# Keeping a decoder's residual stream token-major: activations stationary in the projections that feed it

## The chip, the cores and the metric

The kernel runs on one core of one Trainium2 chip. The core has a matrix engine (TensorE, PE in the profile; its weight loads are listed apart as PEld), a vector engine (VectorE, DVE), an activation engine (ScalarE, ACT), GpSimd (POOL) and a sync engine (SyncE, SP) that here only issues transfers. They run side by side, each through its own queue in order, and wait for each other by semaphores. SBUF is the working memory with 128 partitions; TensorE writes its results to PSUM, eight banks of 128 partitions x 512 f32.

The metric is device time of one execution in microseconds. The profile comes from one execution of its own.

## What is computed

A two-layer decoder trunk on 256 tokens of width 2048, all f32. Cut to the structure:

```python
for i in range(2):
    h = rms_norm(x, attn_norm_w[i])
    if i == 0:
        x = x + mixer_a(h, a_w_qkv, a_w_o)              # stick-breaking attention, 16 heads of 128
    else:
        k, v = shared_kv_blocks(x, kv_norm_w, b_w_kv)   # rms_norm, one projection, rotary on K
        x = x + mixer_b(h, b_w_q, b_w_o, k, v)          # dilated windows, 3 groups of 4 heads
    x = x + conv_ffn(rms_norm(x, ffn_norm_w[i]), w_up, conv_w, conv_b, w_down)   # inner width 5632
    gate = sigmoid(rms_norm(x, ple_norm_w[i]) @ ple_w_gate[i])
    x = x + gate * (p[i] @ ple_w_proj[i])               # p: 256 features per token
return rms_norm(x, final_norm_w)

def rms_norm(x, w):
    return x * rsqrt(mean(x * x, axis=-1) + 1e-6) * w
```

The residual stream is `x`. Four kinds of projection end in it: the attention outputs (`a_w_o`, `b_w_o`), the feed-forward output (`w_down`) and the pair `ple_w_gate`, `ple_w_proj`.

## The kernel before

**Layout.** The stream is held transposed. `x[j]`, j = 0 to 15, is a tile of 128 features on the partitions x 256 tokens; the host hands `x` over transposed and turns the output back. Every activation is held in this form.

**Split operands.** Each f32 operand of a projection is split into a rounded part `hi` (type fp32r) and the rest `lo`. An activation tile `h` holds its hi in columns 0 to 255 and its lo in 256 to 511 (`split_x`, lines 130 to 140, which also multiplies the norm's gain in). A product is hi x hi + hi x lo + lo x hi.

**Weights.** `weights` (line 199) streams the matrix in strips of 512 output features: SP loads raw tiles of up to four blocks of 128 input features (1 MB, four buffers), then ScalarE writes `hi` (line 217) and VectorE `lo` (line 218), two blocks at a time, four buffers each. I call one block of 128 input features of one strip a k-step. `steps` (line 221) sets the order: two k-steps for each output in turn, with the last two k-steps of a strip sorted by output, so that outputs finish one after the other.

**Two forms of a projection.** `strip_t` (line 235) makes transposed results: the weights are stationary, the activations move. For each of four output blocks of 128 features it issues, for each k-step, one matmul with `hi` and 512 columns (line 244, activation hi and lo at once) and one with `lo` and 256 columns (line 247). The bank holds two halves that are added later. `strip_v` (line 265) makes token-major results: the activations are stationary, the weights move. For each of two tiles of 128 tokens it issues, for each k-step, three matmuls of 512 columns (lines 274 to 276) into one bank. Before the change only V used it. A third form, `strip_1` (line 250), is transposed with three matmuls of 256 columns and serves the small `wpp`.

**What follows a projection into the stream.** `add_blocks` (line 492) runs over four strips of `wo_a`, `wo_b` or one half of `wdn`: for each of the four blocks of a strip two VectorE adds into `x[j]` (lines 289 and 290), a square on ScalarE (line 165) added up on VectorE (line 169), and the split of the new block for the next projection. `ple` (line 561) does the gate: `strip_t` on `wpg`, `strip_1` on `wpp`, then `evac` (line 279: copy one half, add the other, multiply by rstd), sigmoid, product, add, square, split. The feed-forward runs in two halves: 6 pairs of up strips, four down strips over 24 k-steps, 5 pairs, four down strips over 20.

**Norm.** `Norm.add` sums squares per partition and token, `done` (line 172) sums over partitions by a matmul with ones (line 176), then Ln, Exp and one Newton step on 128 x 256 give `rstd` spread over all partitions; `column=True` turns it into one value per token on the partitions (line 192) for V. rstd is applied after the next projection.

**Start and end.** `load_x` (line 599) loads two blocks of the transposed stream for every two k-steps of the first strip. `late_loads` (line 114) issues constants on ACT's queue. At the end the last strip of the last gate is followed by the norm, then VectorE and GpSimd multiply eight tiles of 128 x 512 by rstd (line 634), and SP and ACT send them (line 635).

**Order.** The program is written out straight, and a scheduler places each engine's instructions by priority (the written order) and by when it expects their inputs, so that an instruction may go ahead of earlier ones on its engine. The weight splits have raised priority (`AHEAD`). Once placed, each engine's queue is fixed. PSUM: five banks for accumulators (`acc`), one for small products (`att`), a pair (`two`). Activations live in a ring of 42 tiles of 128 x 512.

Of the kernel before, what the change touches and what calls it, by code (L numbers as in the profile page):

```python
# [36 lines left out]
G_ATTN, G_FFN, G_PLE, G_KV, G_FIN = 0, 2 * KB, 4 * KB, 6 * KB, 7 * KB  # L37
V_CONV = 8 * KB
# [29 lines left out]
LAG = 2  # L68
# [5 lines left out]
def tile_trunk(ctx, tc, xT_d, pT_d, pos_d, vec_d, cst_d, csb_d, wqkv, wo_a, wkv, wq_b, wo_b, wup, wdn, wpg, wpp, out_d):  # L74
# [31 lines left out]
    x, x2 = [], []  # L106
    for j0 in range(0, KB, 2):
        t = cst.tile([P, 2, S], F32, name=f"x{j0}")
        x += [t[:, 0, :], t[:, 1, :]]
        x2.append(t)  # L110
# [34 lines left out]

    class Norm:

        def __init__(self):
            self.s = tt("ssum", bufs=2)  # L150
            self.n = 0
            self.rest = []
            self.table = None
# [6 lines left out]
        def add(self, src, apart=False):  # L160
            if self.n == 0:
                nc.scalar.activation(self.s, src, AF.Square)
            else:
                q = tt("sq", tag="t", bufs=6)
                nc.scalar.activation(q, src, AF.Square)
                if apart:
                    self.rest.append(q)
                else:
                    nc.vector.tensor_tensor(self.s, self.s, q, op=OP.add)
            self.n += 1  # L170

        def done(self, column=False):
            ps = bank("nrm")
            qs = [self.s] + self.rest
            for i, q in enumerate(qs):
                nc.tensor.matmul(ps[:, :S], ONE, q, start=i == 0, stop=i == len(qs) - 1)  # L176
            v = tt("nv", tag="t", bufs=6)
            nc.vector.tensor_scalar(v, ps[:, :S], 1.0 / D, EPS, op0=OP.mult, op1=OP.add)
            y = tt("ny", tag="t", bufs=6)
# [3 lines left out]
            t = tt("nt", tag="t", bufs=6)  # L183
# [3 lines left out]
            nc.vector.scalar_tensor_tensor(r, t, 1.5, y, op0=OP.add, op1=OP.mult)  # L187
            if not column:
                return r, None
            pc = bank("ncol")  # L190
            for t in range(2):
                nc.tensor.matmul(
                    pc[:, 2 * t : 2 * t + 1], r[0:1, t * P : (t + 1) * P], ONE[0:1, 0:1], start=True, stop=True
                )
            rc = tt("rcol", (P, 4), bufs=2)
            nc.vector.tensor_copy(rc[:, 0:4:2], pc[:, 0:4:2])
            return r, rc
# [52 lines left out]
    def strip_1(W, s, xs, two):  # L250

        n = len(xs)
        ps = [None] * 2
        a = dict(skip_group_check=True)
        for k, o, hi, lo in (g for group in steps(weights(W, s, n), n, 4) for g in group):
            if k == 0 and o % 2 == 0:
                ps[o // 2] = two[:, o // 2, :]
            c = slice(o * P, (o + 1) * P)
            d = ps[o // 2][:, (o % 2) * S : (o % 2 + 1) * S]
            nc.tensor.matmul(d, lo[:, c], xs[k][:, :S], start=k == 0 and o % 2 == 0, stop=False, **a)  # L260
            nc.tensor.matmul(d, hi[:, c], xs[k][:, S:], start=False, stop=False, **a)  # L261
            nc.tensor.matmul(d, hi[:, c], xs[k][:, :S], start=False, stop=k == n - 1, **a)  # L262
        return [ps[o // 2][:, (o % 2) * S : (o % 2 + 1) * S] for o in range(4)]

    def strip_v(W, s, xs):

        n = len(xs)
        ps = [None] * 2
        for k, t, hi, lo in (g for group in steps(weights(W, s, n), n, 2) for g in group):
# [18 lines left out]
    def add_to_x(j, ps):  # L288
        nc.vector.tensor_tensor(x[j], ps[:, :S], x[j], op=OP.add)  # L289
        nc.vector.tensor_tensor(x[j], ps[:, S:], x[j], op=OP.add)  # L290

    def v_tiles(ps, rc):
        out = []
        for t in range(2):
            v = rt("v")
            nc.scalar.activation(v, ps[t], AF.Copy, scale=rc[:, 2 * t : 2 * t + 1])
# [195 lines left out]
    def add_blocks(W, xs, bases, norm, base=0):  # L492
        out = [[] for _ in bases]
        for s in range(4):
            ps = strip_t(W, s, xs, base=base)
            if norm is None:
                for o in range(4):
                    add_to_x(4 * s + o, ps[o])
                continue
            if s == 3:  # L500
                norm.load_table()
            for o in range(4):
                j = 4 * s + o
                add_to_x(j, ps[o])
                norm.add(x[j])
                for lst, t in zip(out, split_x(x[j], j, bases)):
                    lst.append(t)
        return out

    def ffn(i, xs, rstd):  # L510
# [32 lines left out]
        add_blocks(wdn[i], gs, [], None)  # L543
# [4 lines left out]
        (h,) = add_blocks(wdn[i], gs, [G_PLE + i * KB], norm, base=4 * half)  # L548
# [12 lines left out]
    def ple(i, xs, ps_, rstd, norm, bases=None):  # L561
        out = []
        for s in range(4):
            end = bases is None and s == 3
            if end:
                pr = strip_1(wpp[i], s, ps_, two=two_banks())
            gp = strip_t(wpg[i], s, xs)
            if not end:
                pr = strip_1(wpp[i], s, ps_, two=two_banks())
# [6 lines left out]
            if s == 3 and not end:  # L576
                norm.load_table()
            for o, t in enumerate(ts):
                j = 4 * s + o
                nc.vector.tensor_tensor(t, pr[o], t, op=OP.mult)  # L580
                nc.vector.tensor_tensor(x[j], x[j], t, op=OP.add)
                norm.add(x[j], apart=end)
                if bases is None:
                    if not end:
                        nc.scalar.activation(x[j], x[j], AF.Copy, scale=gain(G_FIN, j))
                else:
                    out += split_x(x[j], j, bases)
        if bases is None:
            norm.load_table()
        return out  # L590
# [8 lines left out]
    def load_x(k0):  # L599
        nc.sync.dma_start(x2[k0 // 2], xT_d[:, k0 : k0 + 2, :])  # L600
# [116 lines left out]
```

## Time and profile before

| | us |
|---|---|
| median of 3 runs | 2391.64 (2391.57 to 2392.1) |
| profiled execution | 2391.75 |
| its span, first to last instruction | 2389.9 |
| mean granted TensorE clock | 0.997 |

Where the stages lie in the span, in us from its start, read from the timeline of PE:

| stage | from | to |
|---|---|---|
| first layer: mixer_a with its projections | 0 | 338 |
| wo_a | 338 | 411 |
| feed-forward | 411 | 1147 |
| ple | 1147 | 1254 |
| second layer: mixer_b with its projections | 1254 | 1462 |
| wo_b | 1462 | 1542 |
| feed-forward | 1542 | 2278 |
| ple | 2278 | 2371 |
| tail | 2371 | 2390 |

How to read the lines shown below: `L244 PE MATMUL acc<-h,whi 128*128 128x512` is line 244, an engine, an operation, the tile written and the tiles read (buffer numbers left out), the stationary operand's size and the moving one's. In the timeline the first column is the start in us, the second the time covered, and `x2` says that two like instructions in a row are merged. A matmul's recorded length goes beyond the start of the next one, so what a matmul costs PE is read from the distance between starts. In groups of instructions the part before the bar names the group and its count, then come busy time and mean ns of one, then the engine's idle time before them and what ended it. In the windows each engine has its busy us and, in brackets, its instructions, in the order PE, PEld, DVE, ACT, POOL; then come granted TensorE clock, DMA share and GB/s.

### The profile page before, as it was taken

To read this page: it belongs to the slowest core of one execution; us is meant where nothing else is said; L and a number is where in the kernel's file an instruction comes from. 1 tells how busy PE (TensorE), PEld (TensorE's weight loads), DVE (VectorE), ACT (ScalarE), POOL (GpSimd) and SP (SyncE) were. 2 spreads that over 40 slices of the span, in tenths; PEclk is the share of its full clock that TensorE was granted. 3 is DMA by queue.
4 is the path that set the end of the run, shared out by engine and by line. 5 is a ranking of instruction groups with operands and counts; after the bars stand their busy time and mean duration, and the time that the engine had idled before them with its cause. 6 is when DMAs were issued, how large, how long until landed. Compare 5 with 4: busy or idle time off the path is not lost.

```text
span 2389.9 us, 34074 instructions
## 1 busy us (share of the span) xinstructions
PE 2366.7 (99%) x13402; PEld 2049.5 (86%) x13402; DVE 1653.5 (69%) x2686; ACT 1283.9 (54%) x1877; POOL 3.6 (0%) x6
## 2 busy tenths in 40 slices
PE   8999999999999999999999999999999999999997
PEld 7888888888888888888888888888888888888886
DVE  8555557777765577766778876777776557776675
ACT  6555545655643455654665444565564345564564
POOL 0000000000000000000000000000000000000000
PEclk9999999999999999999999999999999999999998
DMA  7444455555555555555555444555555555555542
GB/s 279 163 170 167 170 176 188 187 194 188 184 193 193 181 190 193 187 186 191 178 194 191 171 151 164 190 194 188 185 192 193 182 189 194 187 185 192 185 169 105
DMA packets 64001, 439.86 MB, mean 184 GB/s; under 512 B 7232, under 2 KB 7392, under 8 KB 12128
## 3 DMA queue, kind: packets, MB, share of 16 engines
q1 hardware_dynamic: 62352, 435.19, 51.8%
q10 hardware_dynamic: 1488, 2.49, 0.3%
q8 instruction: 105, 1.72, 0.3%
q14 instruction: 56, 0.46, 0.1%
HBM read 435.55 MB, written 2.10 MB: 183 GB/s over the span
## 4 chain that ended last, share of the span: by engine, by line
PE 98%; DVE 1%; ACT 0%; DMA 0%; DVEq 0%; issue 0%; SPq 0%; ACTq 0%
PE acc L244 59%; PE acc L247 29%; PE accv L275 2%; PE accv L274 2%; PE accv L276 2%; PE po L304 1%; PE two L260 0%; PE two L261 0%; PE two L262 0%; PE two L362 0%; PE po L305 0%; PE nrm L176 0%; PE two L446 0%; PE two L376 0%; DMA x<-in_xT 0%; ACT whi L217 0%
## 5 line engine op out<-in xcount | busy, mean ns | idle before, releaser
L218 DVE TENSOR_TENSOR wlo<-raw,whi 128x1024 fp32r<-128x1024 f32 (+1 forms) x825 | 1007.0, 1222 | 650.0 <-ACT whi L217 644.4
L217 ACT ACTIVATE whi<-raw 128x1024 fp32r<-128x1024 f32 (+1 forms) x825 | 871.3, 1058 | 874.1 <-PE acc L244 734.3
L244 PE MATMUL acc<-h,whi 128*128 128x512 f32 x4224 | 1330.5, 396 | 8.1 <-DVE h L136 8.1
L247 PEld LDWEIGHTS acc<-h,wlo 128*128 128x128 f32 x4224 | 793.6, 188 | 186.0
L247 PE MATMUL acc<-h,wlo 128*128 128x256 f32 x4224 | 833.6, 279 | 0.0
L244 PEld LDWEIGHTS acc<-h,whi 128*128 128x128 f32 x4224 | 645.8, 189 | 9.2 <-DVE h L136 8.1
L244 PE MATMUL acc<-g,whi 128*128 128x512 f32 x1408 | 442.2, 396 | 0.0
L247 PEld LDWEIGHTS acc<-g,wlo 128*128 128x128 f32 x1408 | 264.2, 188 | 62.2
L247 PE MATMUL acc<-g,wlo 128*128 128x256 f32 x1408 | 276.4, 278 | 0.0
L244 PEld LDWEIGHTS acc<-g,whi 128*128 128x128 f32 x1408 | 214.7, 189 | 0.5 <-issue 0.4
L244 PE MATMUL acc<-o,whi 128*128 128x512 f32 x448 | 141.4, 397 | 0.0
L281 ACT ACTIVATE c<-acc 128x256 f32<-128x256 f32 x264 | 99.0, 375 | 48.5 <-PE acc L247 48.4
L282 DVE TENSOR_TENSOR c<-acc,c 128x256 f32<-128x256 f32 x264 | 105.1, 418 | 7.7 <-ACT c L281 7.7
L247 PEld LDWEIGHTS acc<-o,wlo 128*128 128x128 f32 x448 | 83.7, 188 | 19.1
L247 PE MATMUL acc<-o,wlo 128*128 128x256 f32 x448 | 88.9, 279 | 0.0
L274 PE MATMUL accv<-whi,h 128*128 128x512 f32 x224 | 88.5, 395 | 0.0
L275 PE MATMUL accv<-wlo,h 128*128 128x512 f32 x224 | 88.4, 394 | 0.0
L276 PE MATMUL accv<-whi,h 128*128 128x512 f32 x224 | 88.1, 393 | 0.0
L284 DVE TENSOR_TENSOR u<-c,rstd 128x256 f32<-128x256 f32 x176 | 71.9, 419 | 0.8
L143 ACT ACTIVATE g<-val 128x256 fp32r<-128x256 f32 x88 | 36.4, 414 | 66.0 <-DVE val L535 66.0
L244 PEld LDWEIGHTS acc<-o,whi 128*128 128x128 f32 x448 | 68.8, 189 | 0.5 <-issue 0.4
L289 DVE TENSOR_TENSOR x<-acc,x 128x256 f32<-128x256 f32 x96 | 38.1, 419 | 33.3 <-PE acc L247 33.3
(146 smaller groups left out, 1283.0 us busy)
## 6 DMA issues: line engine op xcount, KB each, us to landing
raw<-in_wup SPq DMA_DIRECT2D x176, 1024.0 KB, 4.8
raw<-in_wdn SPq DMA_DIRECT2D x88, 1024.0 KB, 4.8
raw<-in_wqkv SPq DMA_DIRECT2D x44, 1024.0 KB, 4.8
raw<-in_wpg SPq DMA_DIRECT2D x32, 1024.0 KB, 4.8
raw<-in_wkv SPq DMA_DIRECT2D x24, 1024.0 KB, 4.7
raw<-in_wo_a SPq DMA_DIRECT2D x16, 1024.0 KB, 4.8
raw<-in_wq_b SPq DMA_DIRECT2D x12, 1024.0 KB, 4.8
raw<-in_wo_b SPq DMA_DIRECT2D x12, 1024.0 KB, 4.8
```

The source lines that it names most:

```text
L143: nc.scalar.activation(h[:, :S], src, AF.Copy)
L217: nc.scalar.activation(hi[:, c], r, AF.Copy)
L218: nc.vector.tensor_tensor(lo[:, c], r, f32(hi[:, c]), op=OP.subtract)
L244: nc.tensor.matmul(ps[o], hi[:, c], xs[k], start=k == 0, stop=False)
L247: nc.tensor.matmul(ps[o][:, S:], lo[:, c], xs[k][:, :S], start=False, stop=k == n - 1)
L274: nc.tensor.matmul(ps[t], xl, hi, start=k == 0, stop=False)
L275: nc.tensor.matmul(ps[t], xh, lo, start=False, stop=False)
L276: nc.tensor.matmul(ps[t], xh, hi, start=False, stop=k == n - 1)
L281: nc.scalar.activation(c, ps[:, S:], AF.Copy)
L282: nc.vector.tensor_tensor(c, ps[:, :S], c, op=OP.add)
L284: nc.vector.tensor_tensor(out, c, rstd, op=OP.mult)
L289: nc.vector.tensor_tensor(x[j], ps[:, :S], x[j], op=OP.add)
```

## The change

The stream is kept as two tiles `x[t]` of 128 tokens on the partitions x 2048 features. The projections into it (`wo_a`, `wo_b`, `wdn`, `wpg`, `wpp`) use `strip_v`; `strip_1` is gone. After each strip of a projection that a norm follows, the new function `turn` transposes the strip on TensorE, eight 128 x 128 f32 transposes into the pair of banks `two`, and the split reads its blocks from there. The first half of `wdn` and the last `ple` have no `turn`.

A norm now sums along the free axis, by the accumulator of the square itself, and its small steps work on 128 x 2. Where the next projection is transposed, `done` spreads rstd by a diagonal matrix and a matmul with ones. The gate takes rstd as the scale of its sigmoid. The final gain, which lies along the free axis now, is loaded spread over the partitions. At the start the stream is loaded twice, transposed into ring tiles for the first projection and token-major into `x`; at the first `ple` copies of the transposed blocks are kept for the shared K/V. The output is token-major.

```diff
+        for t in range(2):
+            nc.scalar.dma_start(x[t], x_d[t])
+        nc.vector.tensor_copy(idf, IDB)
...
+    def strip_of(t, s):
+        return x[t][:, s * 512 : (s + 1) * 512]
...
+        def add(self, s, t):
+            q = tt("sq", (P, 768), tag="e", bufs=1)[:, :512]
+            nc.scalar.activation(q, strip_of(t, s), AF.Square, accum_out=self.s[:, t, s : s + 1])
+
+        def done(self, row=True):
+            small = lambda n: tt(n, (P, 2), bufs=2)
+            v = small("nv")
+            nc.vector.reduce_sum(v, self.s, axis=mybir.AxisListType.X)
+            nc.vector.tensor_scalar(v, v, 1.0 / D, EPS, op0=OP.mult, op1=OP.add)
...
+            rc = small("rcol")
+            nc.vector.scalar_tensor_tensor(rc, t, 1.5, y, op0=OP.add, op1=OP.mult)
+            if not row:
+                return None, rc
+            dg = tt("diag", tag="t", bufs=6)
+            for t in range(2):
+                nc.vector.tensor_scalar(dg[:, t * P : (t + 1) * P], idf, rc[:, t : t + 1], None, op0=OP.mult)
+            ps = bank("nrm")
+            nc.tensor.matmul(ps[:, :S], ONE, dg, start=True, stop=True)
             r = tt("rstd", bufs=2)
+            nc.scalar.activation(r, ps[:, :S], AF.Copy)
+            return r, rc
+
+    def turn(s):
+        two = two_banks()
+        out = []
+        for o in range(4):
+            d = two[:, o // 2, (o % 2) * S : (o % 2 + 1) * S]
             for t in range(2):
+                c = s * 512 + o * P
+                nc.tensor.transpose(d[:, t * P : (t + 1) * P], x[t][:, c : c + P], idf)
+            out.append(d)
+        return two, out
...
-    def add_blocks(W, xs, bases, norm, base=0):
-        out = [[] for _ in bases]
+    def add_strips(W, xs, gain_of, norm, base=0):
+        out = []
         for s in range(4):
-            ps = strip_t(W, s, xs, base=base)
-            if norm is None:
-                for o in range(4):
-                    add_to_x(4 * s + o, ps[o])
-                continue
-            if s == 3:
+            ps = strip_v(W, s, xs, base)
+            if norm is not None and s == 3:
                 norm.load_table()
-            for o in range(4):
-                j = 4 * s + o
-                add_to_x(j, ps[o])
-                norm.add(x[j])
-                for lst, t in zip(out, split_x(x[j], j, bases)):
-                    lst.append(t)
+            for t in range(2):
+                nc.vector.tensor_tensor(strip_of(t, s), ps[t], strip_of(t, s), op=OP.add)
+                if norm is not None:
+                    norm.add(s, t)
+            if norm is not None:
+                for o, b in enumerate(turn(s)[1]):
+                    out += split_x(b, 4 * s + o, [gain_of])
         return out
...
-    def ple(i, xs, ps_, rstd, norm, bases=None):
+    def ple(i, xs, ps_, rc, norm, gain_of=None):
...
-            gp = strip_t(wpg[i], s, xs)
+            gp = strip_v(wpg[i], s, xs)
             if not end:
-                pr = strip_1(wpp[i], s, ps_, two=two_banks())
+                pr = strip_v(wpp[i], s, ps_)
             ts = []
-            for o in range(4):
-                t = tt("pg", tag="t", bufs=6)
-                evac(gp[o], rstd, t)
-                nc.scalar.activation(t, t, AF.Sigmoid)
-                ts.append(t)
+            for t in range(2):
+                g = tt("pg", (P, 768), tag="w", bufs=2)[:, :512]
+                nc.scalar.activation(g, gp[t], AF.Sigmoid, scale=rc[:, t : t + 1])
+                ts.append(g)
...
+            for t, g in enumerate(ts):
+                nc.vector.tensor_tensor(g, pr[t], g, op=OP.mult)
+                nc.vector.tensor_tensor(strip_of(t, s), strip_of(t, s), g, op=OP.add)
+                norm.add(s, t)
+                if gain_of is None:
+                    nc.vector.tensor_tensor(strip_of(t, s), strip_of(t, s), gf[s], op=OP.mult)
+            if gain_of is not None:
+                two, bs = turn(s)
+                for o in range(0, 4, 2):
+                    r = rt("xT")
+                    nc.scalar.activation(r, two[:, o // 2], AF.Copy)
+                    raw += [r[:, :S], r[:, S:]]
+                    for q in range(2):
+                        out += split_x(bs[o + q], 4 * s + o + q, [gain_of])
...
     def load_x(k0):
-        nc.sync.dma_start(x2[k0 // 2], xT_d[:, k0 : k0 + 2, :])
-        for j in (k0, k0 + 1):
-            (h[j],) = split_x(x[j], j, [G_ATTN])
-        for j in range(k0 - LAG, k0 - LAG + 2):
-            if j >= 0:
-                norm.add(x[j])
+        t = rt("xT")
+        nc.sync.dma_start(t.rearrange("p (a b) -> p a b", a=2), xT_d[:, k0 : k0 + 2, :])
+        for q in range(2):
+            (h[k0 + q],) = split_x(t[:, q * S : (q + 1) * S], k0 + q, [G_ATTN])
...
-    r2 = rstd.unsqueeze(1).to_broadcast([P, 2, S])
-    for i, t in enumerate(x2):
-        eng = nc.gpsimd if i % 4 == 3 else nc.vector
-        eng.tensor_tensor(t, t, r2, op=OP.mult)
-        (nc.sync, nc.scalar)[i % 2].dma_start(out_d[:, 2 * i : 2 * i + 2, :], t)
+    for s in range(4):
+        for t in range(2):
+            c = strip_of(t, s)
+            if t == 0:
+                nc.vector.tensor_scalar(c, c, rc[:, t : t + 1], None, op0=OP.mult)
+            else:
+                nc.scalar.activation(c, c, AF.Copy, scale=rc[:, t : t + 1])
+            (nc.sync, nc.scalar)[t].dma_start(out_d[t][:, s * 512 : (s + 1) * 512], c)
```

More of the change, by code (lines that the diff above doesn't have):

```diff
@@ L73, in tile_trunk @@
 @with_exitstack
-def tile_trunk(ctx, tc, xT_d, pT_d, pos_d, vec_d, cst_d, csb_d, wqkv, wo_a, wkv, wq_b, wo_b, wup, wdn, wpg, wpp, out_d):
+def tile_trunk(ctx, tc, xT_d, x_d, pT_d, pos_d, vec_d, cst_d, csb_d, wqkv, wo_a, wkv, wq_b, wo_b, wup, wdn, wpg, wpp, gfin_d, out_d):
     nc = tc.nc
@@ L105, in tile_trunk @@
     vec = cst.tile([P, NVEC], F32, name="vec")
[L106 to L110, printed above, removed]
+    x = [cst.tile([P, D], F32, name=f"x{t}") for t in range(2)]
     c32 = cst.tile([P, NCST], F32, name="c32")
@@ L158, in load_table @@
             tc.keep_in_program_order(self.table)
[L160 to L179, printed above, removed]
+        def add(self, s, t):
[6 more added lines that the diff above has]
+            nc.vector.tensor_scalar(v, v, 1.0 / D, EPS, op0=OP.mult, op1=OP.add)
+            y = small("ny")
             with tc.issue_after(self.table.ins):
@@ L182, in done @@
                 nc.scalar.activation(y, y, AF.Exp, scale=-0.5)
-            t = tt("nt", tag="t", bufs=6)
+            t = small("nt")
             nc.vector.tensor_tensor(t, y, y, op=OP.mult)
             nc.vector.scalar_tensor_tensor(t, t, -0.5, v, op0=OP.mult, op1=OP.mult)
-            r = tt("rstd", bufs=2)
[L187 to L190, printed above, removed]
-            for t in range(2):
[L192 to L197, printed above, removed]
+            rc = small("rcol")
[7 more added lines that the diff above has]
+            nc.tensor.matmul(ps[:, :S], ONE, dg, start=True, stop=True)
+            r = tt("rstd", bufs=2)
+            nc.scalar.activation(r, ps[:, :S], AF.Copy)
[5 more added lines that the diff above has]
+            d = two[:, o // 2, (o % 2) * S : (o % 2 + 1) * S]
+            for t in range(2):
+                c = s * 512 + o * P
+                nc.tensor.transpose(d[:, t * P : (t + 1) * P], x[t][:, c : c + P], idf)
+            out.append(d)
+        return two, out
     def weights(W, s, n, fine=False, before=lambda k0: None, base=0):
@@ L248, in strip_t, with strip_v @@
         return ps
-    def strip_1(W, s, xs, two):
+    def strip_v(W, s, xs, base=0):
         n = len(xs)
         ps = [None] * 2
[L254 to L269, printed above, removed]
+        for k, t, hi, lo in (g for group in steps(weights(W, s, n, base=base), n, 2) for g in group):
             if k == 0:
@@ L547, in ffn @@
         norm = Norm()
-        (h,) = add_blocks(wdn[i], gs, [G_PLE + i * KB], norm, base=4 * half)
+        h = add_strips(wdn[i], gs, G_PLE + i * KB, norm, base=4 * half)
         return h, norm
@@ L576, in ple @@
-            if s == 3 and not end:
-                norm.load_table()
[L578 to L587, printed above, removed]
@@ L593, in tile_trunk @@
+            if gain_of is not None:
[6 more added lines that the diff above has]
+                        out += split_x(bs[o + q], 4 * s + o + q, [gain_of])
+        return out, raw
     idf = cst.tile([P, P], F32, name="idf")
@@ L599, in load_x @@
     def load_x(k0):
-        nc.sync.dma_start(x2[k0 // 2], xT_d[:, k0 : k0 + 2, :])
-        for j in (k0, k0 + 1):
-            (h[j],) = split_x(x[j], j, [G_ATTN])
-        for j in range(k0 - LAG, k0 - LAG + 2):
-            if j >= 0:
-                norm.add(x[j])
+        t = rt("xT")
+        nc.sync.dma_start(t.rearrange("p (a b) -> p a b", a=2), xT_d[:, k0 : k0 + 2, :])
+        for q in range(2):
+            (h[k0 + q],) = split_x(t[:, q * S : (q + 1) * S], k0 + q, [G_ATTN])
     first = strip_t(wqkv, 0, h, True, load_x)
     late_loads()
-    for j in range(KB - LAG, KB):
-        norm.add(x[j])
-    rstd, rc = norm.done(column=True)
+    for t in range(2):
+        for s in range(4):
+            norm.add(s, t)
+    rstd, rc = norm.done()
     o = mixer_a(h, rstd, rc, first)
-    nc.vector.tensor_copy(idf, IDB)
     for i in range(2):
         norm = Norm()
-        (h,) = add_blocks(wo_a if i == 0 else wo_b, o, [G_FFN + i * KB], norm)
+        h = add_strips(wo_a if i == 0 else wo_b, o, G_FFN + i * KB, norm)
         rstd, _ = norm.done()
@@ L703 @@
         "wpp": np.stack([_strips(w) for w in a["ple_w_proj"]]),
+        "gfin": np.ascontiguousarray(a["final_norm_w"]),
     }
@@ L714 @@
     o = r.results[0]["out_0"]
-    return np.ascontiguousarray(o.transpose(2, 1, 0).reshape(1, S, D))
+    return np.ascontiguousarray(o.reshape(1, S, D))
```

53 lines of the change are left out of this document (26 added, 27 removed).

## The prediction

> **What bounds the kernel now.** First the busy shares and the chain of work that ended last, then the waits of PE.
>
> ```profile
> PE 2366.7 (99%) x13402; PEld 2049.5 (86%) x13402; DVE 1653.5 (69%) x2686; ACT 1283.9 (54%) x1877; POOL 3.6 (0%) x6
> PE 98%; DVE 1%; ACT 0%; DMA 0%; DVEq 0%; issue 0%; SPq 0%; ACTq 0%
> ```
>
> ```profile
> PE acc L244 <- DVE h L136: 8.1, 1, 8.1
> PE nrm L176 <- ACT sq L165: 2.5, 2, 1.8
> ```
>
> PE carries the chain and waits for others 10.6 us in all, at the start and at the end. Neither a lighter VectorE nor a lighter ScalarE pays in between: only the number of PE instructions times their spacing counts, plus start and tail. Since recorded matmul durations overlap, I use spacings, the difference of start times in the timeline. First a stretch of L244/L247 pairs (transposed projection; columns: start, us, engine, line), then one of L274 to L276 (activations stationary, already used for V), then the first matmuls after an interruption.
>
> ```profile
> 1000.09 0.63 PE L244 MATMUL acc<-h,whi 128*128 128x512 f32 x2
> ...
> 1009.15 0.62 PE L244 MATMUL acc<-h,whi 128*128 128x512 f32 x2
> ```
>
> ```profile
> 153.29 0.39 PE L276 MATMUL accv<-whi,h 128*128 128x512 f32 x1
> ...
> 158.73 0.39 PE L276 MATMUL accv<-whi,h 128*128 128x512 f32 x1
> ...
> 1408.41 0.39 PE L276 MATMUL accv<-whi,h 128*128 128x512 f32 x1
> ...
> 1410.25 0.39 PE L275 MATMUL accv<-wlo,h 128*128 128x512 f32 x1
> ```
>
> Between the first two rows lie 13 groups of two 512-column and two 256-column matmuls: 9.06/13 = 0.697 us a group. A k-step (one block of 128 input features for four output blocks) is two groups, 1.394 us. Between the next two lie 24 matmuls: 5.44/24 = 0.2267 us each; a k-step of the other form is six, 1.360 us. Both stream 3,072 columns; the first needs eight instructions, the second six. The last pair, eight matmuls in 1.84 us, shows 0.230 us for the first ten or so after an interruption.
>
> **The change part by part.**
>
> *Projections.* The converted strips are those of wdn, wpg, wo_a and wo_b. Each of these transfers brings four k-steps:
>
> ```profile
> raw<-in_wdn SPq DMA_DIRECT2D x88, 1024.0 KB, 4.8
> raw<-in_wpg SPq DMA_DIRECT2D x32, 1024.0 KB, 4.8
> raw<-in_wo_a SPq DMA_DIRECT2D x16, 1024.0 KB, 4.8
> raw<-in_wo_b SPq DMA_DIRECT2D x12, 1024.0 KB, 4.8
> ```
>
> 148 transfers are 592 k-steps. 592 x (1.394 - 1.360) = 592 x 0.0338 (unrounded) = **-20.0 us**. At 0.230 throughout, a k-step would be 1.380 and the gain 8.2 us; I take the settled figure, since these strips are 72 to 144 matmuls with one group of transposes among them, and the row of 24 stands inside an unbroken run of 35.
>
> 0.697 against three times 0.2267 is 17 ns for one instruction fewer on the same 1,536 columns. The Trainium skill (TensorE: Matmul & The Clock Gate, Part 1) puts the fixed cost of a warm matmul at about 2.5 ns; by that, two instructions fewer save 5 ns a k-step, 3 us in all, and the sum below would be +11 instead of -6. The trace disagrees with its 17 ns; the rule is weighed among the rivals.
>
> wpp goes from 24 matmuls of 256 columns a strip to 12 of 512, in 8 strips:
>
> ```profile
> 1162.75 0.28 PE L262 MATMUL two<-p,whi 128*128 128x256 f32 x1
> ...
> 1163.83 0.28 PE L262 MATMUL two<-p,whi 128*128 128x256 f32 x1
> ```
>
> Nine in 1.08 us are 0.120 each: 8 x (24 x 0.120 - 12 x 0.2267) = **-1.3**.
>
> *Transposes.* `turn` runs for four strips of wo_a, wo_b, the second half of wdn in both layers, and the first ple: 20 times eight. The mixer's own f32 transposes show the price, in the midst of L274 to L276:
>
> ```profile
> 1421.14 0.39 PE L275 MATMUL accv<-wlo,h 128*128 128x512 f32 x1
> 1421.38 0.27 PE L482 MATMUL pt<-idf,e 128*128 128x128 f32 x1
> ...
> 1421.59 0.27 PE L484 MATMUL pt<-idf,e 128*128 128x128 f32 x1
> 1421.62 0.48 PE L276 MATMUL accv<-whi,h 128*128 128x512 f32 x1
> 1421.94 0.39 PE L274 MATMUL accv<-whi,h 128*128 128x512 f32 x1
> ```
>
> From L275 to L274 0.80 us pass where two spacings are 0.453: three transposes cost 0.347, with the return to the large matmuls in it; within the group they are 0.105 apart. Eight cost 0.347 + 5 x 0.105 = 0.87; times 20, **+17.4**. Afterwards nine matmuls at 0.230 instead of 0.2267: 0.03 x 20 = **+0.6**.
>
> A transpose waits for VectorE's add to the stream, and behind it on PE's queue stands the next strip, then everything. The order of issue is not the written one: L482 stands between L275 and L276 above, so the scheduler puts a transpose where it expects its input to be ready. How well, the first of the mixer's transposes shows:
>
> ```profile
> 1415.92 0.39 PE L276 MATMUL accv<-whi,h 128*128 128x512 f32 x1
> 1416.41 0.33 PE L482 MATMUL pt<-idf,e 128*128 128x128 f32 x1
> ```
>
> 0.49 instead of 0.227 is a stall of 0.26; the other group had none. So 0 to 0.26 a turn, 0 to 5.2 in all; I take 0.12: **+2.4**. The last turn of a stage is hidden: the next strip has 12 k-steps (16.7 us) before it needs the last four blocks, and add, transposes and split take about 3 to 5 us. Without that cover each of five ends would cost this much.
>
> *Norms.* Seven sums over partitions go; four diagonal products that spread rstd come (start, wo_a, wo_b, first ple).
>
> ```profile
> 32.73 0.39 PE L247 MATMUL acc<-h,wlo 128*128 128x256 f32 x2
> 32.97 0.59 PE L176 MATMUL nrm<-ssum,c 128*128 128x256 f32 x2
> ...
> 33.85 0.40 PE L247 MATMUL acc<-h,wlo 128*128 128x256 f32 x2
> ```
>
> 1.12 us where a group takes 0.70: 0.42 for one. Outside the tail six go and four come, and the two column turns (L192) go, whose price I set at about the same: (4 - 6 - 2) x 0.42 = **-1.7**; bounds -0.8 (L192 free) and -2.5. The vector work shrinks (two adds of 512 columns a strip for eight of 256, no rstd product at the gates) and is hidden by PE either way, as are the four loads of the final gain on ACT's queue, due only once the first strip of the last ple is added.
>
> *Start.* The stream now comes twice: transposed through the ring, and 2 x 1 MB in token rows, issued on ACT's queue behind L117.
>
> ```profile
> 10.00:15.00 5.00, 5.00 (x21) 4.40 (x20) 4.08 (x7) 4.19 (x8) 0.00 (x0) 1.00 1.04 405
> 25.00:30.00 5.00, 5.00 (x30) 4.34 (x30) 5.00 (x10) 3.54 (x9) 0.00 (x0) 1.00 1.03 423
> ```
>
> In these windows (last two columns: DMA share, GB/s) the DMA engines are full. The first strip eats 0.75 MB every 2.79 us, 269 GB/s. 2 MB more take 4.9 us at 410 GB/s; at half the rate each for 10 us the weights come 64 GB/s short, 2.4 us of PE. Bounds 0 (they land in prefetch slack) and 4.9 (all ahead of the weights): **+2.5**. That L169's 15 adds leave a VectorE that is busy 5.00 of 5 us here can only help.
>
> *Tail.* Now 18.6 us pass from the last projection's end to the end of the span, 2389.9:
>
> ```profile
> 2370.92 0.39 PE L247 MATMUL acc<-h,wlo 128*128 128x256 f32 x2
> ...
> 2380.59 5.84 DVE L634 TENSOR_TENSOR x<-x,rstd 128x512 f32<-128x512 f32 x6
> ```
>
> ```profile
> L296 ACT ACTIVATE v<-accv,rcol 128x512 f32<-128x512 f32 x14 | 9.6, 682 | 1.6 <-PE accv L276 1.6
> L157 ACT ACT_TABLE_LOAD x7 | 9.0, 1283 | 0.8 <-PEq L705 0.7
> L455 ACT ACTIVATION_READ_ACCUMULATOR e<-two,nmx 128x1 f32 x24 | 4.7, 195 | 0.0
> L218 DVE TENSOR_TENSOR wlo<-raw,whi 128x512 fp32r<-128x512 f32 x2 | 1.4, 692 | 5.5 <-ACT whi L217 5.5
> L454 DVE TENSOR_SCALAR nmx<-mx 128x1 f32<-128x1 f32 x24 | 3.6, 150 | 0.6
> L480 DVE TENSOR_SCALAR e<-e,co 128x256 f32<-128x256 f32 x12 | 4.2, 350 | 0.0
> ```
>
> After the last matmul come: sigmoid 0.68; table 1.28, beside product and add (2 x 0.69); two squares with their accumulator, 2 x 0.88, to about 3.7; the last gain product to 4.2; five small VectorE and two ScalarE steps, about 1.4, to 5.6; then four strips scaled and sent by each of two engines, VectorE 0.5 to 0.7 each, ScalarE 0.68 plus an issue of 0.3, to about 9.1; then what follows the last scaling now, 2389.9 - 2386.4 = 3.5: 12.6. **-6.0**; bounds -3 (every handover 0.2 us late) and -9 (squares beside the table load, scalings overlapped with issues).
>
> Sum: -20.0 - 1.3 + 17.4 + 0.6 + 2.4 - 1.7 + 2.5 - 6.0 = **-6.1**. The profiled execution took 2391.75 us with a span of 2389.9; less 6.1 it is 2385.65. The median of the runs, 2391.64, lies 0.11 below it: 2385.5, rounded **2385.6**.
>
> **The rivals.**
>
> *The transposes hold PE (slower).* If a turn's first transpose is issued right behind its strip, PE stands for the 0.69 us of the add, and for a weight split (1.22 us, VectorE's longest common operation) where that is ahead: 0.69 to 1.91 a turn, 13.8 to 38.2 in all in place of 2.4. With the middle, 26, the time is 2409. It decides against the change from (6.1 + 2.4)/20 = 0.43 us a turn. For it: PE takes its queue in order, and the add is one step off. Against it: the 0.00 and 0.26 us above. Chance 0.13.
>
> *The matmuls don't settle.* At 0.230 the gain of the projections shrinks from 20.0 to 8.2: 2397.4, just slower. For it: ten matmuls after each interruption are at that spacing. Against it: the long runs. If half of them settle, 2391.5. Chance 0.10, half of it slower.
>
> *The count of instructions saves nothing.* What costs 17 ns may be the change between 512 and 256 columns, or a weight load, and come back in these strips in another shape. At 0.697/3 = 0.2323 a matmul the projections gain 0: 2405.6, slower. Against it: the same weights, split and engine state already give 0.2267 at L274 to L276. Chance 0.02. By the page's 2.5 ns it would be 2402.6.
>
> *Small terms cancel.* Start +4.9, stalls 5.2, tail -3: +8.2 on the sum, 2393.8; with two of the three, about 2391. No difference. Nothing excludes it, as each end has a row behind it. Chance 0.25.
>
> *A transpose costs its record's length.* L484 is recorded at 0.27 us. If PE paid that for each, 160 x 0.27 = 43.2 in place of 17.4: 2411. Spacing 0.105 in the rows speaks against it, and this window of the transposes has granted clock 1.00 (the column after POOL):
>
> ```profile
> 1416.00:1462.00 46.00, 45.90 (x224) 37.14 (x223) 29.27 (x54) 18.94 (x26) 0.00 (x0) 1.00 0.46 159
> ```
>
> Chance 0.02. The Trainium skill (the same page, Part 4: PE-mode transpose) speaks for it: about 275 ns in one kernel's context, and a transpose doesn't count as activity for the clock. The trace agrees with the record's 0.27, not as a price in a row of transposes.
>
> **How the numbers follow.** The forecast as it stands, with its small terms near their values, has 0.48, from 2377 to 2390. By the bound of 0.2% (4.8 us, about what a measurement of this kernel tells from no change) faster is below 2386.9: two thirds or more of the forecast, and its luckier end (-16 with no stall, no start cost, tail -9: 2376), about 0.50 with what the other cases give. Slower is above 2396.4: 0.13 + 0.05 + 0.02 + 0.02, less what of the first lies below, 0.18. The rest, 0.32, is no difference. The range goes from the lucky end to just past the unsettled case, 2377 to 2399; beyond it stay some 0.05 below and 0.14 above.
>
> **What would show it.** In the changed profile: spacing of the strip matmuls in wdn 0.2267 (not 0.230); eight transposes in a group at 0.105 with no more than 0.3 us ahead of them; the first matmul still near 8.1 us and the first strip's end near 32; 12 to 13 us from the last matmul to the end; waits of PE for the stream's add near 2 us in total. It is wrong if PE's waits list the add with tens of us, if the transposes stand 0.2 us apart, or if the first strip ends 5 us late.

## The result, and the profile after

| | before | after |
|---|---|---|
| median, 7 runs each on one chip | 2391.59 (2391.18 to 2392.11) | 2399.31 (2397.34 to 2400.38) |
| profiled execution / its span | 2391.75 / 2389.9 | 2399.31 / 2397.5 |
| mean granted TensorE clock | 0.997 | 0.995 |

The changed kernel takes 1.0031 times as long (95% interval 1.0019 to 1.0042): 7.7 us slower, where 6 us faster was forecast. The busy shares and the chain of the changed kernel, and then its waits of PE (total us, times, longest):

```profile
PE 2363.2 (99%) x12260; PEld 2003.5 (84%) x12260; DVE 1561.1 (65%) x2364; ACT 1271.8 (53%) x1829; POOL 0.2 (0%) x4
PE 97%; ACT 1%; DMA 1%; DVE 1%; issue 0%; SPq 0%; ACTq 0%; DVEq 0%
```

```profile
PE acc L246 <- DVE h L134: 18.8, 5, 7.8
PE acc L249 <- DVE wlo L220: 0.7, 1, 0.7
...
PE two L197 <- DVE x L483: 0.2, 1, 0.2
```

PE is busy 3.5 us less and has 1,142 instructions fewer, as meant. The wait that the prediction feared most, L197's for the stream's add, is 0.2 us in the whole run. What grew is a wait of the first projection, for splits of the transposed stream: 8.1 us in one wait before, 18.8 in five now.

**Where the time went.** PE's timeline has two marks that both kernels share: the first attention scores (L362 before, L345 after) and the start of the last projection matmul.

```profile
57.15 0.59 PE L362 MATMUL two<-qk,qk 128*128 128x256 f32 x2
```

```profile
73.72 0.59 PE L345 MATMUL two<-qk,qk 128*128 128x256 f32 x2
...
2383.17 0.39 PE L263 MATMUL accv<-whi,h 128*128 128x512 f32 x1
```

Before, the second mark is the second of the two L247 that start at 2370.92, at 2371.04. So:

| part of the span | before | after | difference | forecast |
|---|---|---|---|---|
| start to first scores (head) | 57.15 | 73.72 | +16.6 | +2.1 |
| first scores to last projection matmul (middle) | 2313.9 | 2309.45 | -4.4 | -2.2 |
| from there to the end (tail) | 18.9 | 14.3 | -4.5 | -6.0 |

The forecast column is the prediction's own terms, put where they lie: its start term in the head, with -0.4 for the first norm, whose sum and column turn lie there (L176 at 32.97, L192 at 37.24); -20.0 - 1.3 + 17.4 + 0.6 + 2.4 - 1.3 in the middle. Middle and tail together gave 8.9 us, about what was forecast (8.2). The head alone turned the sign.

**What happened in the head.** From the transfers that SP issues in the first 40 us, before (L209 a weight, L600 two blocks of the stream):

```profile
...
1.65 0.42 SPq L600 DMA_DIRECT2D x<-in_xT  x1
2.12 0.43 SPq L209 DMA_DIRECT2D raw<-in_wqkv  x1
2.59 0.65 SPq L600 DMA_DIRECT2D x<-in_xT  x1
...
16.09 0.43 SPq L600 DMA_DIRECT2D x<-in_xT  x1
```

and after (L211 a weight, L591 the stream), with SP's largest wait in the first 60 us (total, times, longest):

```profile
...
1.64 0.42 SPq L591 DMA_DIRECT2D xT<-in_xT  x1
2.10 1.04 SPq L211 DMA_DIRECT2D raw<-in_wqkv  x2
5.12 0.33 SPq L591 DMA_DIRECT2D xT<-in_xT  x1
5.50 6.42 SPq L211 DMA_DIRECT2D raw<-in_wqkv  x4
14.09 0.33 SPq L591 DMA_DIRECT2D xT<-in_xT  x1
...
17.67 0.33 SPq L591 DMA_DIRECT2D xT<-in_xT  x1
...
27.59 0.42 SPq L591 DMA_DIRECT2D xT<-in_xT  x1
...
38.49 0.90 SPq L591 DMA_DIRECT2D xT<-in_xT  x2
```

```profile
SPq L211 <- DVE wlo L220: 34.7, 9, 9.1
```

Before, weight and stream loads alternate and the eighth stream load is out at 16.09. After, the scheduler put the second one behind two more weights, the third behind four, and so on. A weight load waits until VectorE's `wlo` frees a raw buffer; a stream load that needs no buffer stands behind it in SP's queue. The last leave at 38.49. PE then lacks activations while its weights lie ready:

```profile
17.55 1.22 PE L246 MATMUL acc<-h,whi 128*128 128x512 f32 x2 [4.93 <-DVE h L134]
...
21.56 0.80 PE L246 MATMUL acc<-h,whi 128*128 128x512 f32 x2
...
30.70 1.65 PE L246 MATMUL acc<-h,whi 128*128 128x512 f32 x3 [4.08 <-DVE h L134]
...
35.80 0.59 PE L184 MATMUL nrm<-diag,c 128*128 128x256 f32 x2
```

The brackets are idle time and what ended it. The idle time has a second price: after 4.93 us of it three groups take 4.01 us (17.55 to 21.56) in place of 3 x 0.697 = 2.09, after 4.08 us four take 5.10 (30.70 to 35.80) in place of 2.79. The windows show why (busy us of PE, PEld, DVE, ACT, POOL, then granted clock, DMA share, GB/s):

```profile
15.00:20.00 5.00, 2.45 (x7) 2.05 (x8) 2.02 (x3) 1.64 (x3) 0.00 (x0) 0.51 1.02 412
...
30.00:35.00 5.00, 4.30 (x13) 3.72 (x14) 2.73 (x11) 2.68 (x9) 0.00 (x0) 0.50 0.99 405
```

The granted clock is 0.51 and 0.50. The Trainium skill (TensorE: Matmul & The Clock Gate, Part 1) says that PE falls to half its clock after an idle window of about 3.4 us and regains it after as long a busy one; the trace agrees for idles of 4.93 and 4.08 us. Other runs give no length below which an idle is safe: in e8, below, one of 2.57 us was followed by half clock too, while in e3 the clock stayed at 1.00 after one of 2.80 us.

The head's account: waits 18.8 + 0.7 + 0.2 (one for `whi`) - 8.1 = 11.6 more; half clock 1.9 + 2.3 = 4.2. Against that, PE's first four groups, which start at half speed in both kernels (the first eight matmuls of 512 columns stand 0.45 us apart), took 4.8 us in place of 5.3, 0.5 less. So 1.3 of the 16.6 is not assigned.

### The profile page after: what moved, and what is told of

It reads as the page before. It is cut to its first block, busy times and chain, and to the rows that moved or that the text cites. A ratio compares the mean times of both kernels' runs of the same rounds, so it can differ in the third digit from the quotient of the medians.

```text
span 2397.5 us, 31193 instructions
## 1 busy us (share of the span) xinstructions
PE 2363.2 (99%) x12260; PEld 2003.5 (84%) x12260; DVE 1561.1 (65%) x2364; ACT 1271.8 (53%) x1829; POOL 0.2 (0%) x4
## 4 chain that ended last, share of the span: by engine, by line
PE 97%; ACT 1%; DMA 1%; DVE 1%; issue 0%; SPq 0%; ACTq 0%; DVEq 0%
PE acc L246 35%; PE acc L249 18%; PE accv L262 14%; PE accv L261 14%; PE accv L263 14%; PE two L197 1%; PE po L287 1%; DMA xT<-in_xT 1%; ACT whi L219 0%; DVE wlo L220 0%; DMA vec<-in_vec 0%; PE two L345 0%; PE po L288 0%; PE two L429 0%; PE two L359 0%
## 5 line engine op out<-in xcount | busy, mean ns | idle before, releaser
L246 PE MATMUL acc<-h,whi 128*128 128x512 f32 x3712 | 1174.8, 398 | 19.0 <-DVE h L134 18.8
L249 PEld LDWEIGHTS acc<-h,wlo 128*128 128x128 f32 x3712 | 698.8, 189 | 164.1 <-DVE wlo L220 1.1
L249 PE MATMUL acc<-h,wlo 128*128 128x256 f32 x3712 | 733.8, 279 | 0.7 <-DVE wlo L220 0.7
L262 PE MATMUL accv<-wlo,g 128*128 128x512 f32 x704 | 274.6, 390 | 0.0
L263 PE MATMUL accv<-whi,g 128*128 128x512 f32 x704 | 274.5, 390 | 0.0
L261 PE MATMUL accv<-whi,g 128*128 128x512 f32 x704 | 274.1, 389 | 0.0
L261 PE MATMUL accv<-whi,h 128*128 128x512 f32 x480 | 188.5, 393 | 0.0
L262 PE MATMUL accv<-wlo,h 128*128 128x512 f32 x480 | 188.5, 393 | 0.0
L263 PE MATMUL accv<-whi,h 128*128 128x512 f32 x480 | 188.1, 392 | 0.0
L263 PEld LDWEIGHTS accv<-whi,g 128*128 128x128 f32 x704 | 132.5, 188 | 26.9
L261 PEld LDWEIGHTS accv<-whi,g 128*128 128x128 f32 x704 | 132.2, 188 | 27.2
L262 PEld LDWEIGHTS accv<-wlo,g 128*128 128x128 f32 x704 | 132.2, 188 | 27.1
L263 PEld LDWEIGHTS accv<-whi,h 128*128 128x128 f32 x480 | 90.3, 188 | 17.8
L261 PEld LDWEIGHTS accv<-whi,h 128*128 128x128 f32 x480 | 90.2, 188 | 17.5
```

Source lines behind the costliest of these rows:

```text
L246: nc.tensor.matmul(ps[o], hi[:, c], xs[k], start=k == 0, stop=False)
L249: nc.tensor.matmul(ps[o][:, S:], lo[:, c], xs[k][:, :S], start=False, stop=k == n - 1)
L261: nc.tensor.matmul(ps[t], xl, hi, start=k == 0, stop=False)
L262: nc.tensor.matmul(ps[t], xh, lo, start=False, stop=False)
L263: nc.tensor.matmul(ps[t], xh, hi, start=False, stop=k == n - 1)
```

## The experiments

The theory: **SP's order** makes the head late. Its rival: the **second copy** of the stream, 2 MB of token rows, takes the DMA engines from the weights, as the prediction priced it. Beside them stood the question whether the **transposes** cost more than their spacing says. In all diffs "..." leaves something out; ratios are to the kernel before on the same chip.

### Order restored: e1_order

In the changed kernel each weight load of the first strip is issued behind the stream load that precedes it in the text. `issue_after` ties an instruction to another's place on the queue; the rest is unchanged.

```diff
-                nc.sync.dma_start(raw[...], W[...])
+                with tc.issue_after(xdma[0]) if fine and xdma[0] is not None else nullcontext():
+                    nc.sync.dma_start(raw[...], W[...])
...
-        nc.sync.dma_start(t.rearrange(...), xT_d[:, k0 : k0 + 2, :])
+        xdma[0] = nc.sync.dma_start(t.rearrange(...), xT_d[:, k0 : k0 + 2, :]).ins
```

> The changed kernel, with one thing undone: in the first strip each weight load on SP's queue is issued behind the transposed-stream load of the two blocks before it, so that weights and stream alternate as before the change; the 2 MB of token rows still load early on ACT's queue. Theory A (the order on SP's queue: stream loads stand behind weight loads that wait for a free buffer) expects the head, the time to the first attention scores, to fall from 73.7 us to 58 to 62 us and the whole from 2399.3 to 2384 to 2389. Theory B (the 2 MB fill the DMA engines) expects the head to stay above 68 us and the whole above 2393.

2387.04 us (2386.25 to 2389.26), ratio 0.9981 (0.9972 to 0.9990). First scores at 61.16, 12.6 earlier than in the changed kernel; the whole 12.3 faster. The waits of PE:

```profile
PE acc L249 <- DVE h L134: 10.1, 3, 7.9
PE nrm L184 <- DVE diag L182: 1.6, 2, 1.3
...
```

Behind the first groups the granted clock is 1.00 in every window of 4 us, from 12 to 40. So the order alone was worth some 12 of the 16.6 us, and the change with its start in order is faster than the kernel before.

### Rows late: e2_late_rows and e3_both

The token rows are loaded only behind the first strip's last split of the stream. e2 leaves SP's queue to the scheduler, e3 has the order of e1 as well.

```diff
-        for t in range(2):
-            nc.scalar.dma_start(x[t], x_d[t])
...
+            last[0] = nc.scalar.activation(h[:, :S], src, AF.Copy, scale=gain(b, j)).ins
...
+    with tc.issue_after(last[0]):
+        for t in range(2):
+            nc.scalar.dma_start(x[t], x_d[t])
```

> The changed kernel, but the 2 MB of token rows are issued only after the last split of the first strip's activations on ScalarE; the order on SP's queue is left to the scheduler, which still puts some weight loads ahead of stream loads (third stream load behind four weight loads in place of six). Theory B (contention with the 2 MB) expects the head at 57 to 60 us and the whole at 2383 to 2386. Theory A (order) expects only a part of the gain, since the order mends only in part: head 62 to 70 us, whole 2388 to 2396.

> Both edits together: weights and stream alternate on SP's queue, and the 2 MB of token rows come after the first strip's splits. Both theories expect the head at 57 to 59 us, as before the change, and the whole at 2382 to 2385. If the head stays above 62 us, neither is the whole cause, and the norm at the start (its squares on ScalarE now come in one block) would be next.

e2: 2394.51 (2392.74 to 2398.14), ratio 1.0013 (1.0003 to 1.0022). Its stream loads still stand behind weights (1.65, 5.38, 7.32, 12.79 up to 27.79), and PE waits for them:

```profile
PE acc L246 <- DVE h L134: 12.6, 3, 8.0
```

First scores at 72.45 in its profile, whose execution lies at the top of that range. e2 is 4.8 us faster than the changed kernel, but not by the rows alone: the scheduler put its third stream load behind two weights instead of four. e3: 2386.75 (2385.66 to 2390.86), ratio 0.9981 (0.9972 to 0.9991), first scores at 61.86; its waits in the first 62 us, without three smaller ones of 1.7 us together:

```profile
PE acc L249 <- DVE h L134: 8.1, 1, 8.1
PE nrm L184 <- DVE diag L182: 2.8, 1, 2.8
...
```

Without the rows PE waits for the stream once and for 8.1 us, as before the change; but then the rows, and with them the first norm, come late, and the time is that of e1, above the 2382 to 2385 that both theories had expected. With the rows moved and the order left, the time stays above before's; with the order put right, moving them gains nothing measurable. The second copy is the smaller cause.

### What displaces the order: t5_ring_landing

The kernel before, with one thing of the change: the transposed stream lands in tiles of the activation ring, and VectorE copies it into its place. No token rows, no transposes.

```diff
-        nc.sync.dma_start(x2[k0 // 2], xT_d[:, k0 : k0 + 2, :])
+        t = rt("xT")
+        t3 = t.rearrange("p (a b) -> p a b", a=2)
+        nc.sync.dma_start(t3, xT_d[:, k0 : k0 + 2, :])
...
-            (h[j],) = split_x(x[j], j, [G_ATTN])
+            (h[j],) = split_x(t3[:, j - k0], j, [G_ATTN])
...
+        nc.vector.tensor_copy(x2[k0 // 2], t3)
```

> The kernel before the change, with one part of the change alone: the transposed stream lands in ring tiles, the splits read it there, and VectorE copies it to its place. No token rows are loaded. With this alone the scheduler puts weight loads ahead of stream loads on SP's queue. Theory A (order) expects the first scores at 64 to 72 us in place of 57.2 and the whole at 2398 to 2406, with no 2 MB in play. If the order does not matter, only the eight copies count, at 0.3 to 0.5 us each on a busy VectorE: first scores at 57 to 60, whole 2392 to 2395.

2402.05 (2400.57 to 2402.84), ratio 1.0043 (1.0027 to 1.0058). Stream loads at 1.65, 6.06, 8.08, 13.12, 17.65, 19.92, 23.34 and 26.27, first scores at 67.38, PE's wait:

```profile
PE acc L244 <- DVE h L136: 13.2, 3, 8.8
```

So landing in ring tiles, with the copies that it asks for here, is enough to have the stream loads displaced, and the run loses 10 us without a second copy of the stream from HBM. The eight copies take VectorE 0.42 us each and are in these 10 us; the changed kernel has none of them. Why the scheduler places a load into a ring tile later is not settled by a run.

### The displaced order in the kernel before: e8_order_before

The other way about: the kernel before with its second stream load bound behind two more weight transfers and the third behind four more, as in the changed kernel; the later ones are not held beyond that.

```diff
+    UPTO = {0: 0, 2: 4, 4: 12}
...
+            for ka in range(0, min(n, 1 + (UPTO.get(k0, n) if fine else k0)), size):
+                if ka not in raws:
+                    fetch(ka)
...
-        nc.sync.dma_start(x2[k0 // 2], xT_d[:, k0 : k0 + 2, :])
+        with tc.issue_after(rdma[0]):
+            nc.sync.dma_start(x2[k0 // 2], xT_d[:, k0 : k0 + 2, :])
```

> The kernel before the change, everything as it was, but the issue order on SP's queue in the first strip is forced: the second stream load behind the third weight load and the third behind the seventh, as in the changed kernel; the later ones follow at once. Theory A expects first scores at 62 to 72 us and the whole at 2396 to 2406. If the head of the changed kernel came from the 2 MB or from its norm, nothing moves: 2391 to 2393.

2398.12 (2395.23 to 2399.37), ratio 1.0024 (1.0014 to 1.0033). SP's queue and PE's wait:

```profile
4.32 8.20 SPq L214 DMA_DIRECT2D raw<-in_wqkv  x4
12.58 0.50 SPq L617 DMA_DIRECT2D x<-in_xT  x1
...
14.75 2.66 SPq L617 DMA_DIRECT2D x<-in_xT  x5
```

```profile
PE acc L260 <- DVE h L136: 11.0, 2, 8.4
```

The order alone slows the old kernel by 6.4 us in the median. The head of its profiled execution (2395.72, near the low end of its range) grew by 4.0 us to 61.17, less than expected: here five stream loads leave at once at 14.75, where the changed kernel held its last four until 27.59 to 38.49. After the second of the two idles, 2.57 us long, PE ran at half clock for a while (the third column from the end is the granted clock):

```profile
20.00:24.00 4.00, 4.00 (x19) 3.49 (x18) 1.69 (x4) 2.71 (x6) 0.00 (x0) 0.69 1.05 403
```

The kind of loss is shown, the full size of it not.

### The price of a transpose: e6_turn_twice

Each `turn` issues its eight transposes twice, into the same places; the rest is the changed kernel.

```diff
-        for o in range(4):
+        for o in 2 * list(range(4)):
...
-        return two, out
+        return two, out[:4]
```

> The changed kernel with every strip's eight transposes issued twice into the same banks, 160 transposes more. If a transpose costs PE its spacing, 0.105 us, the time grows by 160 x 0.105 = 16.8 us, to 2416. If the price of a turn lies in the waits and interruptions around the group, and not in the transposes, it grows by less than 5 us.

2415.27 (2414.13 to 2416.42, two runs), ratio 1.0098 (1.0078 to 1.0119), 16.0 above the changed kernel. A turn in the changed kernel, and the same in e6:

```profile
1068.56 0.39 PE L262 MATMUL accv<-wlo,g 128*128 128x512 f32 x1
1068.78 0.33 PE L197 MATMUL two<-idf,x 128*128 128x128 f32 x1
1068.87 0.48 PE L263 MATMUL accv<-whi,g 128*128 128x512 f32 x1
1069.18 0.40 PE L261 MATMUL accv<-whi,g 128*128 128x512 f32 x1
1069.41 0.95 PE L197 MATMUL two<-idf,x 128*128 128x128 f32 x7
1070.12 0.48 PE L262 MATMUL accv<-wlo,g 128*128 128x512 f32 x1
1070.44 0.39 PE L263 MATMUL accv<-whi,g 128*128 128x512 f32 x1
```

```profile
1070.13 0.40 PE L261 MATMUL accv<-whi,g 128*128 128x512 f32 x1
1070.37 1.82 PE L197 MATMUL two<-idf,x 128*128 128x128 f32 x15
1071.95 0.47 PE L262 MATMUL accv<-wlo,g 128*128 128x512 f32 x1
```

The transpose that needs only the first token tile goes ahead, the other seven follow two matmuls later; neither stands. Over all turns the first interruption costs 0.178 us and the second 0.798: 0.976 together. In e6 the second costs 1.669, so eight more take 0.871, 0.109 each. The middle of e6's profile, from first scores at 71.11 to the last matmul at 2397.99, is 2326.9, 17.4 above 2309.45: 160 x 0.109 again. (Its head came out 2.6 us shorter than that of the changed kernel, at the same code.)

### Rows in the middle, and one group a turn: e5, e7, e9, e10, e11

What was left over is the rows' place and the first, single transpose. e5 is e1 with the rows issued behind the fourth pair of splits. e7 is e5 with `for t in (1, 0)` in `turn`, so that the first transpose in order needs the last add and all eight go together. e9 is e3, and e11 is e1, with that loop. e10 has that loop too, the rows behind the fifth pair, and the squares of the first norm held behind the last split.

```diff
+        if k0 == ROWS_AT:
+            with tc.issue_after(last[0]):
+                for t in range(2):
+                    nc.scalar.dma_start(x[t], x_d[t])
...
-            for t in range(2):
+            for t in (1, 0):
```

> The changed kernel with weights and stream alternating on SP's queue, and the 2 MB of token rows issued in the middle of the first strip, behind the fourth pair of splits on ScalarE: late enough not to delay the first stream loads, early enough that the start norm does not hold PE (it did for 2.8 us with the rows at the end). First scores at 57.5 to 60 us, whole 2382.5 to 2386; faster than the kernel before by 6 to 9 us. If the 2 MB cost bandwidth wherever they stand, first scores stay at 61 to 62 and the whole at 2386 to 2387.

> The run with rows in the middle, and each turn's transposes start with the second token tile, so that the first of them waits for the last add and the eight stand in one group instead of one and seven. The trace has 0.18 + 0.80 = 0.98 us for the two pieces; one group of eight should take 0.87 plus up to 0.1 of wait: 20 x 0.1 = 2 us less than the run it builds on. If the wait for the add grows instead, it is the same or slower.

> Alternating order on SP's queue, token rows after the first strip's splits, and transposes that start with the second token tile. The run with both head edits took 2386.75 us; one group in place of one and seven took 3.1 us off the run with the rows in the middle. Expected 2383.5 to 2385, faster than the kernel before by 6.5 to 8 us.

> As the run with the rows in the middle and one group, but the rows one pair later and the start norm's squares held on ScalarE's queue behind the last split of the first strip. If the rows in the middle were dear because the squares, waiting for the second row transfer, stood ahead of weight splits on ScalarE's queue (4.9 us in the trace), first scores come to 58 to 61 us and the whole to 2382 to 2385. If it was their bandwidth, first scores stay at 62 to 66 and the whole at 2387 to 2390.

> Alternating order on SP's queue and one group of transposes, the token rows early as in the change. The run with the order alone took 2387.04; less 2 to 3 us for the groups: 2384 to 2385. Faster than the kernel before by 6.5 to 8 us.

| | us | ratio (interval) | first scores | middle |
|---|---|---|---|---|
| e5, rows in the middle | 2392.51 (2386.69 to 2394.78) | 0.9999 (0.9990 to 1.0008) | 65.80 | 2309.4 |
| e7, with one group | 2389.41 (2385.11 to 2391.28) | 0.9988 (0.9979 to 0.9996) | 62.31 | 2307.7 |
| e9, e3 with one group | 2385.93 (2383.80 to 2387.37) | 0.9975 (0.9965 to 0.9984) | 61.94 | 2307.6 |
| e11, e1 with one group | 2385.63 (2384.97 to 2386.81) | 0.9975 (0.9965 to 0.9985) | 61.68 | 2307.6 |
| e10, squares last | 2384.04 (2382.96 to 2386.77) | 0.9967 (0.9955 to 0.9979) | 63.08 | 2307.55 |

e5 came out 6.5 us above the upper end of what was expected. Its rows reach ScalarE's squares before the last weights are split, and a square that waits for its row blocks the weight split behind it:

```profile
31.00 0.63 ACT L162 ACTIVATE sq<-x 128x512 f32<-128x512 f32 x1 [4.90 <-DMA x<-in_x]
31.63 1.04 ACT L223 ACTIVATE whi<-raw 128x1024 fp32r<-128x1024 f32 x1
```

This is the same fault as SP's, on another queue: work that is ready stands behind work that waits. The time now also varies from run to run by up to 8 us. e10 takes the squares out of the way and has the lowest median of all, though its interval overlaps those of e9 and e11. It doesn't settle what made e5 dear: its median lies where the squares were expected to be the cause, but its first scores, at 63.08 in a profiled execution at the top of its range (2386.77), lie where they were expected with bandwidth as the cause; there ScalarE waits 5.45 us for a weight to land (L223, up to 31.95). One group a turn is worth 1.7 to 1.9 us in the middle (2309.4 in e5, 2309.5 in e1 and e3, about 2307.6 with it). The medians of e9 and e11 fell by 0.8 and 1.4 us, to just above what was expected of them. A turn of e11:

```profile
1056.96 0.39 PE L265 MATMUL accv<-wlo,g 128*128 128x512 f32 x1
1057.19 1.04 PE L197 MATMUL two<-idf,x 128*128 128x128 f32 x8
1057.99 0.48 PE L266 MATMUL accv<-whi,g 128*128 128x512 f32 x1
1058.30 0.39 PE L264 MATMUL accv<-whi,g 128*128 128x512 f32 x1
```

1.34 us less two spacings of 0.2267 is 0.89 for eight transposes, in place of 0.976 for one and seven.

## Why the prediction was wrong

**Start: the step that failed.** It gave +2.5, with bounds of 0 and 4.9, from bytes over bandwidth alone, and took the order of SP's queue as it was in the old trace. The head measured +16.6. Landing the stream in ring tiles moved its loads behind weight loads that wait for buffers (t5: +10 us with no other part of the change, its copies included); undoing the displacement gave 12.3 us back (e1). What the step did price, the second copy, fits in size: with the order restored the head is 61.16, 4.0 above before, inside the bounds. There PE waits 10.1 us for the stream, 8.1 in e3 with the rows late, and another 1.3 us of the head go to the first norm (L184). It followed the rows onto ACT's queue, but not the transposed loads (L600, now L591) through SP's, although their destination had changed. It had a case for small terms that cancel, and a sign of its own for this fault (the first strip late by 5 us), but no rival in which the head costs more than 4.9.

**Projections: right.** The strips of `wdn` run at the settled spacing:

```profile
700.33 0.39 PE L263 MATMUL accv<-whi,g 128*128 128x512 f32 x1
...
711.89 0.39 PE L263 MATMUL accv<-whi,g 128*128 128x512 f32 x1
```

51 spacings in 11.56 us are 0.2267 each, and so is the mean over the run of 576. The rival in which the matmuls don't settle at that falls. So does the one in which the count of instructions saves nothing, and with it, in these strips, the fixed cost of 2.5 ns that the Trainium skill (TensorE: Matmul & The Clock Gate, Part 1) gives: taken alone it would have left the middle, as an estimate, a loss of some 15 us, and the middle gained.

**Transposes and their stalls: right in sum, the parts exchanged.** Forecast 0.87 + 0.12 a turn, measured 0.976. There is no stall; the scheduler splits the turn into one and seven instead, which costs 0.09 more than eight together (0.89 in e11), near the 0.12 that the stall was put at. The two rivals on the transposes fall: PE waits 0.2 us for the add, and eight more transposes take 0.871 us, not 8 x 0.27.

**Middle as a whole.** -4.4 against -2.2. With the turns at 20 x 0.976 = 19.5 for 19.8, some 1.9 us of gain are assigned to no term; the norms, with bounds from -0.8 to -2.5, were not measured by themselves.

**Tail: right in kind, 1.5 us short.** From the last projection matmul on, cut to the steps that set the end:

```profile
2383.59 0.69 ACT L562 ACTIVATE pg<-accv,rcol 128x512 f32<-128x512 f32 x1 [0.67 <-PE accv L263]
...
2390.94 1.33 ACT L623 ACTIVATE x<-x,rcol 128x512 f32<-128x512 f32 x2 [0.45 <-ACT x L623]
2391.69 1.64 ACTq L624 DMA_DIRECT2D out<-x  x2
```

The last scaling ends at 2392.27, 9.1 us after that matmul's start, as forecast. What follows it was mis-sized: 5.2 us to the end of the span where 3.5 was taken from the old trace. ScalarE issues its own sends behind its scalings, the last issue ends at 2393.33, and the end comes 4.2 us after that; in the old trace it came 3.1 after the last send's issue.

**The sum.** With its own terms and a head of +4.0, as measured in e1, the forecast would have been about 2387.4; e1, the change with its start in order, took 2387.04. That it comes so close is in part luck, since a middle 2.2 better and a tail 1.5 worse than forecast nearly cancel. So the argument about PE held, and the queue that it did not follow decided. One of its sums is off: the three terms named for the lucky end (no stall, no start cost, tail -9) give -14.0, not -16; nothing here depends on it.

Open remain: why the scheduler places the loads into ring tiles late; 1.3 us of the head; 1.9 us of the middle; what made the rows in the middle dear; and why e8 loses less in its head than the changed kernel.

## What to carry to other kernels

A load that moves to another buffer may move in its queue as well: after every change, read the queue of the issuing engine from the start of the span and look for work that is ready behind work that waits for a buffer. Price a start not by bytes alone but by the time at which each input can leave, and add the time at half clock that can follow an idle of PE (here 1.9 and 2.3 us lost after idles of 4.93 and 4.08). A gain of a per mille that is counted over thousands of matmuls is lost in one badly ordered strip at the start.

## What the hardware showed beside that

An f32 transpose of 128 x 128, recorded at 0.27 us, costs PE 0.105 to 0.109 in a row of them; breaking into a run of 512-column matmuls a second time costs some 0.09 us more (0.976 for 1 + 7, 0.89 for 8). An idle of PE of 2.57 us was enough for a stretch at half clock in e8, and one of 2.80 was not in e3. The last send's way to the end of the span differed by 1.1 us between two kernels that write the same 2 MB (3.1 before, 4.2 after).
